# Moving the expert table ahead of the row pick, and a first-freed list of weight buffers, in a transformer block with 32 experts

## The chip, the cores and the metric

The kernel runs on one core of a Trainium2 chip. The metric is the device time of one execution in microseconds. The core's engines are named as in the profile: PE (TensorE, matrix products), DVE (VectorE), ACT (ScalarE), POOL (GpSimd) and SP (SyncE, which here only issues transfers).

## What is computed

Two blocks follow one another on 512 tokens of width 1024, in float32. The first is two layers of windowed attention with a pooling mixer and a gated feed-forward; the second is a recurrent mixer and then a mixture of experts. The change is in the mixture of experts:

```
x = layer_norm(ALPHA * x + mix, ln1_g, ln1_b)
grp = argmax(x @ w_group + b_group)                 # 1 of 4 groups, for each token
top_p, top_i = top_k(softmax(logits of the group's 8 experts), 2)
weights = p_group * top_p / sum(top_p)              # 2 experts for each token
# rows of each expert e, in blocks of up to 128 tokens:
y = (silu(xs @ w1[e]) * (xs @ w3[e])) @ w2[e]       # 1024 -> 512 -> 1024
x = layer_norm(ALPHA * x + sum of weighted y, ln2_g, ln2_b)
```

The three matrices of an expert are 2 MB each, so that the 32 experts hold 201 MB, all of which are read once.

## The kernel before

The first 2000 us compute everything up to the mixer's last product, `mix_out`. It also transposes the result into token rows `XU` (four tiles of 128 tokens), and it issues the loads of the first experts' weights (`prefetch`). `logits` makes the router's scores, `norm1` normalises `XU` on ACT and writes the rows to DRAM (`xs`), `route` chooses the experts.

`route` counts the tokens of each expert, ranks the experts by their count (`perm`, `rr`), and so gets the table `eid`, which says which expert has which rank. Two experts are fixed: ranks 0 and 1 always go to experts 0 and 1 (`NS = 2`), whose weights can therefore be loaded before any token is routed. The other weights are loaded through registers that SP reads from `eid`. Then `table` makes the list of tokens for each expert's 128 places (`tb`), and `weights` the factors of these tokens (`sw`). A large tile R, one-hot over places, is the stationary operand of both.

The experts are worked in 15 units (`UNITS`): ranks 0 to 3 alone, ranks 4 to 19 in pairs of up to 64 tokens, ranks 20 to 31 in fours of up to 32 tokens. Each unit fills the 128 columns of TensorE, so that each takes the same products, while it needs 6, 12 or 24 transfers of 1 MB. `ORDER` is the order of the units. A step of `experts` does, for the next unit n and the present unit u: transposes of n's rows (`xt`), gate product of n (`gu`), `ht` and the down product of u (`yp`), first half of n's up product, `combine` of u into `XU` (`yc`), second half of the up product. Rows of later units come from DRAM by an indirect transfer from POOL (`gather`). The rows of unit 0 are not gathered: `pick`, a 0/1 matrix, is the moving operand of 64 short products (32 in the code, two passes each) with `XU` stationary, which give the rows already transposed; `x_parts` scales them.

Weight tiles (`ew`, 1 MB each) come from pools of several tags. `SLOTS` lists 15 buffers, which are used in turn; the norm's two vectors take one of them until `scale_x` has used them. A phase `rx` holds the tiles of `extra`, a second table for experts with more tokens than their places; after unit 1 that phase is closed, two buffers "n" are opened in its memory, and 17 buffers are used in turn from then on. SP issues the loads in program order, each one as soon as its buffer is free and no more than eight are in flight. The scheduler of the framework orders the other engines' instructions by priority and expected readiness.

After the sixth unit, `overflow` is a loop over the blocks that did not find a place, with a count read at run time. It is empty with these inputs, but all engines go through its entry. Before it, `prefetch` issues transfers for all buffers but one.

Of the kernel before, what the change touches and what calls it, by code (L numbers as in the profile page):

```python
# [20 lines left out]
S = 512  # L21
# [1338 lines left out]
class K3(K2):  # L1360
# [46 lines left out]
    def mix_out(self, H, MH):  # L1407
# [17 lines left out]
        self.tokens(U[7], 7)  # L1425

    def logits(self):
        nc, v = self.nc, self.nc.vector
        T = lambda name, *s: self.ph.tile([128, *s], F32, name=name)
        lt = T("lt", 512)  # L1430
# [29 lines left out]
    def route(self, L):  # L1460
# [39 lines left out]
        self.warm(m, 8)  # L1500
# [8 lines left out]
        xu = self.XU.rearrange("s b (p k) -> s b k p", k=8)  # L1509

        def pick(t, g):
            for b in range(4):
                for i in range(4):
                    nc.tensor.matmul(t[:, i * 128:(i + 1) * 128], lhsT=xu[:, b, 4 * g + i, :], rhs=S[:, b, :],
                                         start=(b == 0 and i == 0), stop=(b == 3 and i == 3))

        X = self.x_parts(pick)

        C = self.keep.tile([128, 5, NE], F32, name="C")
        with self.tc.issue_after(last.ins):  # L1520
# [19 lines left out]
            for n, d in ((SOLO, 64.0), (HALF, 32.0)):  # L1540
# [16 lines left out]
            R, V, V0 = T("R", 8, 128, dt=F32R), T("V", 8, NT, dt=F32R), T("V0", 8, NT)  # L1557
# [3 lines left out]
            v.tensor_tensor(R, iota[:, None, :].to_broadcast([128, 8, 128]), lane[:, :, None].to_broadcast([128, 8, 128]),  # L1561
                            op=OP.is_equal)
# [5 lines left out]
        return X, ga, OH, C  # L1568

    def table(self, R, V, n, nm):  # L1570
# [3 lines left out]
        for i in range(8):  # L1574
            nc.tensor.matmul(p[:, :n], lhsT=R[:, i, :], rhs=V[:, i, :], start=(i == 0), stop=(i == 7))
# [3 lines left out]
        v.tensor_copy(tokf, tok)  # L1579
        return tok, tokf  # L1580

    def slot_weights(self, V0, R, n, nm):

        nc, v = self.nc, self.nc.vector
        w = self.ph.tile([128, 8, n], F32, name="wv" + nm)
        V = self.ph.tile([128, 8, 2, n], F32R, name="wV" + nm)
        h, l = V[:, :, 0, :], V[:, :, 1, :]
# [4 lines left out]
        for i in range(8):  # L1592
            nc.tensor.matmul(p[:, 0:2 * n], lhsT=R[:, i, :], rhs=V[:, i].rearrange("p a b -> p (a b)"), start=(i == 0), stop=(i == 7))
# [5 lines left out]
    def scale_x(self):  # L1599

        gb = [self.part(self.wp["r", "ln1_g_2", "ln1_b_2"], c, D) for c in (0, D)]
        for t in range(4):
            x = self.XU[:, t, :]
            self.nc.vector.scalar_tensor_tensor(x, x, ALPHA, gb[0], op0=OP.mult, op1=OP.mult)
            self.nc.vector.scalar_tensor_tensor(x, gb[1], ALPHA, x, op0=OP.mult, op1=OP.add)

    def weights(self, L, gm, em, V0, R):

        nc, v = self.nc, self.nc.vector
        T = lambda name, *s: self.ph.tile([128, *s], F32, name=name)  # L1610
# [13 lines left out]
        return self.slot_weights(V0, R, NT, "m")  # L1624

    def extra(self, OH, C):

        v = self.nc.vector
        T = lambda name, *s, dt=F32: self.ph.tile([128, *s], dt, name=name)
# [31 lines left out]
        for th in (256.0, 384.0):  # L1661
# [5 lines left out]
        ob1, V, R = T("obx", 8, NX), T("Vx", 8, NX, dt=F32R), T("Rx", 8, 128, dt=F32R)  # L1667
# [4 lines left out]
        v.tensor_tensor(R, iota[:, None, :].to_broadcast([128, 8, 128]), rk[:, :, None].to_broadcast([128, 8, 128]),  # L1672
                        op=OP.is_equal)
        self.xtok, self.xtokf = self.table(R, V, NX, "x")
        self.xws = self.slot_weights(ob1, R, NX, "x")
        yield
        xe, xb, xo = T("xe", NX, NE), T("xb", NX, NE), T("xo", NX)
        io = iota[:, 0:NX, None].to_broadcast([128, NX, NE])
        v.tensor_tensor(xe, io, ovb[:, None, :].to_broadcast([128, NX, NE]), op=OP.is_ge)
        v.tensor_tensor(xb, io, inc[:, None, :].to_broadcast([128, NX, NE]), op=OP.is_lt)  # L1680
        yield
        v.tensor_tensor(xe, xe, xb, op=OP.mult)
        v.tensor_tensor(xe, xe, iota[:, None, 0:NE].to_broadcast([128, NX, NE]), op=OP.mult)
        v.reduce_sum(xo, xe, axis=AX.X)
# [18 lines left out]
    def moe_setup(self):  # L1703
# [15 lines left out]
        self.seq = sum((seq(u, w) for u, w in ((0, 0), (0, 1), (1, 0), (0, 2), (1, 1), (1, 2))), [])  # L1719
        self.seq.append(("r", "ln1_g_2", "ln1_b_2"))  # L1720
# [8 lines left out]
        self.slots = sum(([k] * n for k, n in SLOTS.items()), [])  # L1729
        self.wp, self.nld, self.ev = {}, 0, {}  # L1730

    TAGS = dict(b="rawb", r="raw", w="w", m="m", n="n")
# [28 lines left out]
    def prefetch(self, n=None):  # L1761

        n = self.static if n is None else min(n, len(self.seq))
        while self.nld < n:
            k = self.seq[self.nld]
            r = self.wp[k] = self.slot()
# [6 lines left out]
    def weight(self, u, w):  # L1773

        ks = [(u, w, s, j) for s in range(2) for j in range(UNITS[u][1])]
        self.prefetch(self.seq.index(ks[-1]) + 1)
        return lambda s, j: self.wp[u, w, s, j]
# [37 lines left out]
    def product(self, X, u, m, p=None, ks=range(KB)):  # L1815

        p = p or self.ps("gu")
        w = self.weight(u, m)
# [225 lines left out]
```

## Time and profile before

| | us |
|---|---|
| median of 3 runs | 2572.79 |
| lowest and highest of them | 2572.56, 2578.59 |
| the profiled execution | 2578.66 |
| its span, from the first instruction to the last | 2576.8 |

The span is divided in 40 slices of 64.4 us in the page's slices. Times in the rows are counted from the span's start. The experts begin near 2035 us.

### The profile page before, as it was taken

How to read it: one execution, taken by the hardware profiler on the slowest of the kernel's cores; microseconds unless marked ns; L12 is line 12 of the kernel's file. 1: busy time of each engine (PE TensorE's matmuls, PEld its weight loads, DVE VectorE, ACT ScalarE, POOL GpSimd, SP SyncE). 2: the span in 40 equal slices, each digit the busy share in tenths (PEclk: the TensorE clock that was granted, in tenths of full speed). 3: DMA queues.
4: the chain of work that ended last, by engine and by line, in shares of the span. 5: the costliest groups of instructions: out<-in, count | busy, mean ns of one | idle time of the engine just before them, and what ended most of it. 6: DMA issues, size and time to landing. Idle time of an engine off the chain costs nothing. (4 is left out here: it accounts for less than half of the span.)

```text
span 2576.8 us, 30602 instructions
## 1 busy us (share of the span) xinstructions
PE 2420.7 (94%) x11847; PEld 1774.4 (69%) x11847; DVE 1366.5 (53%) x2190; ACT 906.9 (35%) x1582; POOL 362.7 (14%) x354
## 2 busy tenths in 40 slices
PE   7999999999999999998999999999999888959996
PEld 4678777778788888887878787888887643323332
DVE  4867576437976233346878875455654631122224
ACT  3654232233764222234555554333432211111211
POOL 1334000005342000003423330000000000000000
PEclk9998999999999999999999999999999999979998
DMA  7541675431212332323112222222225469999996
GB/s 254 184 130 57 213 270 196 149 97 51 70 50 74 106 98 83 97 65 99 42 58 74 63 69 93 89 73 89 66 90 208 172 210 420 421 373 420 419 421 253
DMA packets 221295, 416.60 MB, mean 162 GB/s; under 512 B 11619, under 2 KB 185167, under 8 KB 193500
## 3 DMA queue, kind: packets, MB, share of 16 engines
q1 hardware_dynamic: 215472, 408.17, 44.2%
q0 software_dynamic: 2016, 3.73, 0.4%
q10 hardware_dynamic: 3660, 2.72, 0.4%
q8 instruction: 94, 1.54, 0.2%
q14 instruction: 53, 0.43, 0.0%
HBM read 414.01 MB, written 4.19 MB: 162 GB/s over the span
## 5 line engine op out<-in xcount | busy, mean ns | idle before, releaser
L149 DVE TENSOR_TENSOR w<-raw,w 128x1024 fp32r<-128x1024 f32 (+2 forms) x216 | 262.0, 1214 | 231.6 <-ACT w L148 231.6
L148 ACT ACTIVATE w<-raw 128x1024 fp32r<-128x1024 f32 (+2 forms) x228 | 229.0, 1010 | 376.6 <-PE pu L158 148.0
L156 PE MATMUL pj<-Hh,w 128*128 128x512 f32 (+1 forms) x704 | 281.8, 404 | 6.0 <-ACT Hh L392 3.6
L157 PE MATMUL pj<-Hl,w 128*128 128x512 f32 (+1 forms) x704 | 277.7, 396 | 7.4 <-DVE Hl L395 6.8
L158 PE MATMUL pj<-Hh,w 128*128 128x512 f32 (+1 forms) x704 | 274.4, 391 | 0.0
L1812 PE MATMUL gu<-ew,x 128*64 128x512 f32 (+2 forms) x1008 | 238.0, 610 | 7.0 <-DMA ew<-in_w 6.9
L156 PE MATMUL po<-Gh,w 128*128 128x512 f32 (+1 forms) x608 | 212.4, 350 | 0.5 <-ACT Gh L621 0.5
L158 PE MATMUL po<-Gh,w 128*128 128x512 f32 (+1 forms) x608 | 212.1, 349 | 0.0
L157 PE MATMUL po<-Gl,w 128*128 128x512 f32 (+1 forms) x608 | 211.3, 347 | 0.0
L156 PE MATMUL pu<-Hh,w 128*128 128x512 f32 (+1 forms) x448 | 172.1, 384 | 0.2
L158 PE MATMUL pu<-Hh,w 128*128 128x512 f32 (+1 forms) x448 | 170.0, 380 | 0.0
L157 PE MATMUL pu<-Hl,w 128*128 128x512 f32 (+1 forms) x448 | 170.0, 379 | 0.0
L1812 PEld LDWEIGHTS gu<-ew,x 128*64 128x64 f32 (+2 forms) x1008 | 73.1, 136 | 138.7 <-issue 122.9
L157 PEld LDWEIGHTS pj<-Hl,w 128*128 128x128 f32 x704 | 134.9, 192 | 43.4 <-DVE Hl L395 9.7
L158 PEld LDWEIGHTS pj<-Hh,w 128*128 128x128 f32 x704 | 134.3, 191 | 36.6 <-issue 7.7
L156 PEld LDWEIGHTS pj<-Hh,w 128*128 128x128 f32 x704 | 134.5, 193 | 34.7 <-ACT Hh L392 4.7
L1857 DVE SCALAR_TENSOR_TENSOR yl<-yp,wsm,yh 128x512 fp32r<-128x512 f32 x30 | 22.5, 750 | 253.5 <-ACT yh L1856 251.7
L157 PE MATMUL pg<-Hl,w 128*128 128x512 f32 (+1 forms) x384 | 147.2, 384 | 6.7 <-DVE Hl L395 6.6
L156 PE MATMUL pg<-Hh,w 128*128 128x512 f32 (+1 forms) x384 | 147.6, 385 | 0.0
L158 PE MATMUL pg<-Hh,w 128*128 128x512 f32 (+1 forms) x384 | 146.4, 381 | 0.0
L1812 PE MATMUL yp<-ew,hT 128*64 128x512 f32 (+2 forms) x512 | 128.2, 596 | 13.2 <-ACT hT L1838 7.4
L1088 POOL TENSOR_TENSOR QP<-QP,tot 128x512 f32<-128x512 f32 x64 | 102.9, 1611 | 220.9 <-ACT Y L1081 174.5
(508 smaller groups left out, 4763.4 us busy)
## 6 DMA issues: line engine op xcount, KB each, us to landing
ew<-in_w SPq DMA_DIRECT2D x192, 1024.0 KB
raw<-in_w_in SPq DMA_DIRECT2D x34, 1024.0 KB
raw<-in_ada_w SPq DMA_DIRECT2D x24, 1024.0 KB
raw<-in_w_gate SPq DMA_DIRECT2D x22, 1024.0 KB
raw<-in_w_up SPq DMA_DIRECT2D x22, 1024.0 KB
raw<-in_ada_w SPq DMA_DIRECT2D x40, 512.0 KB
raw<-in_w_in SPq DMA_DIRECT2D x40, 512.0 KB
raw<-in_w_down SPq DMA_DIRECT2D x16, 1024.0 KB
```

The lines of the kernel that those rows point to most:

```text
L148: nc.scalar.activation(hv[:, k], rv[:, k], AF.Copy)
L149: (nc.gpsimd if b in self.low else nc.vector).tensor_tensor(lv[:, k], rv[:, k], hv[:, k].bitcast(F32), op=OP.subtract)
L156: nc.tensor.matmul(out, lhsT=wh, rhs=ah, start=first, stop=False)
L157: nc.tensor.matmul(out, lhsT=wh, rhs=al, start=False, stop=False)
L158: return nc.tensor.matmul(out, lhsT=wl, rhs=ah, start=False, stop=last)
L1088: nc.gpsimd.tensor_tensor(w, w, self.other(TOT, h, seg=1), op=OP.mult)
L1812: self.plast = self.nc.tensor.matmul(out[n * j:n * j + n, :], lhsT=X[k // 4][:, k % 4 * 128 + n * j:k % 4 * 128 + n * j + n], rhs=w, start ...
L1857: v.scalar_tensor_tensor(lo, p, ws, hi.bitcast(F32), op0=OP.mult, op1=OP.subtract)
```

## The change

The rows of unit 0 are now picked by 8 products (16 passes) with `pick` stationary and 512 columns of `XU` moving; ACT copies the result to the row buffer `XG[0]`, and the transposes that other units use follow (`x_transpose`). In the program the tables stand ahead of this. The norm's vectors get four tiles of the tag "H" instead of a weight buffer, and so do R (two halves), `lt` and the tiles of `extra`; its phase `rx` is gone. The tag "m" has three buffers, and one "n" is opened when the routing is over. Weight buffers are given out from a list, in the order in which they were freed, and are put on it after each half of a product. The order of the units puts the two fours 12 and 13 behind units 0 and 1. `extra` runs in six steps per unit. Before the loop all 17 buffers are filled.

```diff
-ORDER = (0, 1, 12, 2, 13, 3, 4, 5, 6, 7, 8, 9, 10, 11, 14)
+ORDER = (0, 12, 1, 13, 2, 3, 4, 5, 6, 7, 8, 9, 10, 11, 14)
-SLOTS = dict(b=6, r=3, w=4, m=2)
+FIRST = ["rawb"] * 5 + ["raw"], ["raw"] * 2 + ["w"] * 4
+FREE = ["rawb"] + ["m"] * 3
...
+        self.gb = [self.blk("H", F32, "gb") for _ in range(4)]
+        for i, t in enumerate(self.gb):
+            src = A[("ln1_g_2", "ln1_b_2")[i // 2]]
+            nc.sync.dma_start(t, bass.AP(tensor=src.tensor, offset=src.offset + i % 2 * 512, ap=[[0, 128], [1, 512]]))
...
-        self.warm(m, 8)
+        self.warm(m, 12)
...
-                    nc.tensor.matmul(t[:, i * 128:(i + 1) * 128], lhsT=xu[:, b, 4 * g + i, :], rhs=S[:, b, :],
-                                         start=(b == 0 and i == 0), stop=(b == 3 and i == 3))
-
-        X = self.x_parts(pick)
...
+            R, V, V0 = self.onehot(lane), T("V", 8, NT, dt=F32R), T("V0", 8, NT)
...
-        ga = self.product(X, 0, 0, self.ps("ga", "mod"))
-        with self.tc.issue_after(self.xlast.ins), self.tc.issue_after(self.plast.ins):
             self.tok, self.tokf = self.table(R, V, NT, "m")
             self.ws = self.weights(L, gm, em, V0, R)
+        for i in range(2):
+            p = self.ps("xp")
+            c = slice(i * 512, (i + 1) * 512)
+            for b in range(4):
+                self.plast = nc.tensor.matmul(p, lhsT=S[:, b, :], rhs=self.XU[:, b, c], start=(b == 0), stop=(b == 3))
+            nc.scalar.activation(self.XG[0][:, c], p, AF.Copy)
+        X = self.x_transpose(self.XG[0])
+        with self.tc.issue_after(self.tlast.ins):
             self.scale_x()
...
+    def onehot(self, lane):
+
+        R = []
+        for i in range(2):
+            R.append(self.blk("H", F32R, "R", (128, 4, 128)))
+            self.nc.vector.tensor_tensor(R[i], self.cm[:, None, 0:128].to_broadcast([128, 4, 128]),
+                                         lane[:, 4 * i:4 * i + 4, None].to_broadcast([128, 4, 128]), op=OP.is_equal)
+        return lambda i: R[i // 4][:, i % 4, :]
...
-        self.seq = sum((seq(u, w) for u, w in ((0, 0), (0, 1), (1, 0), (0, 2), (1, 1), (1, 2))), [])
-        self.seq.append(("r", "ln1_g_2", "ln1_b_2"))
+        self.seq = [k for u in range(NS) for w in range(3) for k in seq(u, (0, 1, 2)[w])]
...
-        self.slots = sum(([k] * n for k, n in SLOTS.items()), [])
+        self.free = [s for f in FIRST for s in f] + FREE
...
-    def slot(self):
-
-        self.slots.append(self.slots.pop(0))
-        return self.blk(self.TAGS[self.slots[-1]], F32, "ew", (128, 2048))
+    def slot(self, k=None):
+
+        self.at[k] = self.free.pop(0)
+        return self.blk(self.at[k], F32, "ew", (128, 2048))
+
+    def used(self, u, w, s):
+
+        self.free += [self.at[u, w, s, j] for j in range(UNITS[u][1])]
...
-    def experts(self, X, ga, later, out):
+    def experts(self, X, later, out):
...
-        sub, hT = ExitStack(), None
-        sub.enter_context(self.phase("rx"))
+        hT = None
+        self.free.append("n")
         self.gather(XG[1], col(self.tok, 1))
-        h = self.hidden(ga, self.product(X, 0, 1))
+        h = self.hidden(self.product(X, 0, 0), self.product(X, 0, 1))
...
-            if i < 2:
-                for _ in range(8 if i == 0 else 99):
-                    next(later, None)
-            if i == 1:
-                sub.close()
-                sub.enter_context(self.phase("m2", n=2))
-                self.slots[:0] = ["n", "n"]
+            for _ in range(6):
+                next(later, None)
             if i == QOV:
-                self.prefetch(self.nld + len(self.slots) - 1)
+                self.prefetch(self.nld + len(self.free))
...
-            with self.phase("mo", m=2, HT=1):
+            with self.phase("mo", m=3, HT=1):
...
+                with self.phase("mn", n=1):
+                    self.experts(X, self.extra(*x), out)
```

## Rows read from the trace of the kernel before

**Rows 1.** The page: bytes moved in each slice, and the count of weight transfers.
```profile
GB/s 254 184 130 57 213 270 196 149 97 51 70 50 74 106 98 83 97 65 99 42 58 74 63 69 93 89 73 89 66 90 208 172 210 420 421 373 420 419 421 253
...
ew<-in_w SPq DMA_DIRECT2D x192, 1024.0 KB
```
**Rows 2.** Windows: busy us (instructions) of PE, PEld, DVE, ACT, POOL; clock, DMA share, GB/s.
```profile
2020.00:2030.00 10.00, 10.00 (x43) 10.00 (x44) 0.96 (x4) 1.50 (x4) 0.00 (x0) 1.00 0.00 0
2080.00:2090.00 10.00, 7.68 (x30) 4.63 (x29) 4.33 (x7) 3.38 (x9) 0.99 (x1) 1.00 0.83 302
2100.20:2118.00 17.80, 17.80 (x131) 7.71 (x124) 6.34 (x13) 0.60 (x1) 0.00 (x0) 1.00 0.23 77
2118.00:2294.00 176.00, 136.08 (x532) 52.80 (x530) 31.81 (x52) 21.92 (x49) 2.97 (x3) 0.91 1.00 412
2296.00:2548.20 252.20, 238.17 (x1097) 91.15 (x1095) 63.80 (x103) 42.74 (x96) 6.33 (x7) 0.99 1.00 411
```
**Rows 3.** Timeline of SP: start, duration from first issue to last, count.
```profile
1953.04 47.39 SPq L1759 DMA_DIRECT2D ew<-in_w  x12
2007.70 0.43 SPq L1692 DMA_DIRECT2D ew<-in_ln_b  x1
...
2036.45 64.07 SPq L1759 DMA_DIRECT2D ew<-in_w  x16
...
2117.97 156.65 SPq L1759 DMA_DIRECT2D ew<-in_w  x68
...
2295.90 0.34 SPq L1759 DMA_DIRECT2D ew<-in_w  x1
```
**Rows 4.** SP's waits from 2036 to 2125: us in total, times, longest.
```profile
SPq L1749 <- DVE cap L1539: 18.6, 1, 18.6
SPq L1759 <- PE sw L1593: 16.8, 1, 16.8
```
**Rows 5.** SP's waits from 2255 to 2305, around the loop.
```profile
SPq L1922 <- SPq L1922: 19.2, 5, 9.3
```
**Rows 6.** Timeline of PE at the loop's exit; in brackets its idle time before.
```profile
2294.93 1.97 PE L1803 MATMUL xt<-cst,xg 128*128 128x128 f32 x8 [25.03 <-SPq L1922]
```
**Rows 7.** Timeline of PE and DVE from the pick to unit 1's rows.
```profile
2017.49 1.90 PE L1457 MATMUL warm<-onesb 128*128 128x512 bf16 x8
2019.50 15.48 PE L1514 MATMUL xt<-pick,xu 128*128 128x128 f32 x64
...
2035.05 0.40 PE L1530 MATMUL rr<-cst,rank 32*128 32x32 f32 x2
2035.38 7.13 PE L1812 MATMUL ga<-ew,x 128*128 128x512 f32 x16
...
2047.96 1.36 PE L1575 MATMUL tb<-V,R 128*128 128x16 f32 x8
2049.17 1.04 PE L1593 MATMUL sw<-wVm,R 128*128 128x32 f32 x8
...
2056.79 1.97 PE L1803 MATMUL xt<-cst,xg 128*128 128x128 f32 x8 [5.62 <-DMA xg<-xs,tokm]
...
2020.13 0.23 DVE L1527 TENSOR_SCALAR perm<-cm,rank 32x32 f32<-32x32 f32 x1
...
2035.49 0.18 DVE L1534 CAST eid<-rr 1x32 int32<-1x32 f32 x1 [1.86 <-PE rr L1530]
...
2037.13 1.22 DVE L1604 SCALAR_TENSOR_TENSOR xu<-xu,ew 128x1024 f32<-128x1024 f32 x1
...
2049.77 0.18 DVE L1579 CAST tfm<-tokm 128x16 f32<-128x16 int32 x1
```
**Rows 8.** Chain of waits, one unit of the stretch behind the loop: start, us, what.
```profile
2324.35 1.09 PE xt L1803 x8
...
2333.22 0.60 ACT hT L1838
...
2353.32 1.09 PE xt L1803 x8
```

More of the change, by code (lines that the diff above doesn't have):

```diff
@@ L1592, in slot_weights @@
         for i in range(8):
-            nc.tensor.matmul(p[:, 0:2 * n], lhsT=R[:, i, :], rhs=V[:, i].rearrange("p a b -> p (a b)"), start=(i == 0), stop=(i == 7))
+            nc.tensor.matmul(p[:, 0:2 * n], lhsT=R(i), rhs=V[:, i, :], start=(i == 0), stop=(i == 7))
         ws = self.keep.tile([128, n], F32, name="ws" + nm)
@@ L1599, in scale_x @@
     def scale_x(self):
-        gb = [self.part(self.wp["r", "ln1_g_2", "ln1_b_2"], c, D) for c in (0, D)]
         for t in range(4):
-            x = self.XU[:, t, :]
-            self.nc.vector.scalar_tensor_tensor(x, x, ALPHA, gb[0], op0=OP.mult, op1=OP.mult)
-            self.nc.vector.scalar_tensor_tensor(x, gb[1], ALPHA, x, op0=OP.mult, op1=OP.add)
+            for i in range(2):
+                x = self.XU[:, t, i * 512:(i + 1) * 512]
+                self.nc.vector.scalar_tensor_tensor(x, x, ALPHA, self.gb[i], op0=OP.mult, op1=OP.mult)
+                self.nc.vector.scalar_tensor_tensor(x, self.gb[2 + i], ALPHA, x, op0=OP.mult, op1=OP.add)
     def weights(self, L, gm, em, V0, R):
         nc, v = self.nc, self.nc.vector
-        T = lambda name, *s: self.ph.tile([128, *s], F32, name=name)
+        T = lambda name, *s, dt=F32: self.ph.tile([128, *s], dt, name=name)
         ex, z, d, r = T("ex", 4, 4), T("z", 4), T("dd", 4), T("rr", 4)
@@ L1623, in weights, with T @@
         v.tensor_tensor(W[:, :, 1], W[:, :, 0], d, op=OP.mult)
-        return self.slot_weights(V0, R, NT, "m")
+        return self.slot_weights(V0, R, NT, "m", T)
     def extra(self, OH, C):
         v = self.nc.vector
-        T = lambda name, *s, dt=F32: self.ph.tile([128, *s], dt, name=name)
+        st = {}
+        def T(name, *s, dt=F32):
+            n = math.prod(s)
+            t, o = st.get(dt, (None, 512))
+            if o + n > 512:
+                t, o = self.blk("H", dt, name), 0
+            st[dt] = t, o + n
+            t = t[:, o:o + n]
+            return t.rearrange("p (a b) -> p a b", b=s[-1]) if len(s) == 2 else t
         iota, val, cnt = self.cm[:, 0:128], self.cm[:, 256:264], C[:, 4, :]
@@ L1671, in extra @@
         v.tensor_tensor(V, ob1, val[:, :, None].to_broadcast([128, 8, NX]), op=OP.mult)
-        v.tensor_tensor(R, iota[:, None, :].to_broadcast([128, 8, 128]), rk[:, :, None].to_broadcast([128, 8, 128]),
-                        op=OP.is_equal)
+        R = self.onehot(rk)
         self.xtok, self.xtokf = self.table(R, V, NX, "x")
-        self.xws = self.slot_weights(ob1, R, NX, "x")
+        self.xws = self.slot_weights(ob1, R, NX, "x", T)
         yield
[L1677 to L1684, printed above, removed]
+        xo = T("xo", NX)
+        for h in range(0, NX, 16):
+            xe, xb = T("xe", 16, NE), T("xb", 16, NE)
+            io = iota[:, h:h + 16, None].to_broadcast([128, 16, NE])
+            v.tensor_tensor(xe, io, ovb[:, None, :].to_broadcast([128, 16, NE]), op=OP.is_ge)
+            v.tensor_tensor(xb, io, inc[:, None, :].to_broadcast([128, 16, NE]), op=OP.is_lt)
+            v.tensor_tensor(xe, xe, xb, op=OP.mult)
+            v.tensor_tensor(xe, xe, iota[:, None, 0:NE].to_broadcast([128, 16, NE]), op=OP.mult)
+            v.reduce_sum(xo[:, h:h + 16], xe, axis=AX.X)
+            yield
         self.xtab = self.keep.tile([128, NX + 1], I32, name="xtab")
@@ L1771, in prefetch, with weight @@
             self.nld += 1
-    def weight(self, u, w):
-        ks = [(u, w, s, j) for s in range(2) for j in range(UNITS[u][1])]
+    def weight(self, u, w, s):
+        ks = [(u, w, s, j) for j in range(UNITS[u][1])]
         self.prefetch(self.seq.index(ks[-1]) + 1)
-        return lambda s, j: self.wp[u, w, s, j]
+        return [self.wp[k] for k in ks]
     def gather(self, xg, col):
@@ L1817, in product @@
         p = p or self.ps("gu")
-        w = self.weight(u, m)
         for k in ks:
-            W = [self.part(w(k // 4, j), k % 4 * 512) for j in range(UNITS[u][1])]
+            W = [self.part(r, k % 4 * 512) for r in self.weight(u, m, k // 4)]
             self.rowmm(p, X, k, W, k == 0, k == KB - 1)
+            if k % 4 == 3:
+                self.used(u, m, k // 4)
         return p
@@ L1842, in down @@
         ps = [self.ps("yp"), self.ps("yp")]
-        w = self.weight(u, 2)
         for k in range(4):
             for i in range(2):
-                W = [self.part(w(k // 2, j), k % 2 * D + i * 512) for j in range(UNITS[u][1])]
+                W = [self.part(r, k % 2 * D + i * 512) for r in self.weight(u, 2, k // 2)]
                 self.rowmm(ps[i], h, k, W, k == 0, k == 3)
+            if k % 2:
+                self.used(u, 2, k // 2)
         return ps
@@ L2008, in moe @@
                     self.norm1()
-                    X, ga, *x = self.route(L)
-                self.experts(X, ga, self.extra(*x), out)
+                    X, *x = self.route(L)
+                with self.phase("mn", n=1):
+                    self.experts(X, self.extra(*x), out)
     def run(self, out, ctx):
```

35 lines of the change are left out of this document (11 added, 24 removed).

## The prediction

> **What bounds the kernel now.** I read the page's slices first [rows 1]: the DMA engines are loaded through the last sixth of the span, at some 420 GB/s, while before it they swing between 42 and 270. That last sixth is the 32 experts. The windows by stretch [rows 2] show what to see in it: from 2118 to 2294 and from 2296 to 2548 the engines move 412 and 411 GB/s with a share of 1.00, but from 2020 to 2030 nothing at all, and from 2100 to 2118 only 77 GB/s. So the experts are bound by the transfer of weights wherever it runs, and the question is where it doesn't run. The page counts 192 transfers of 1024 KB, and the SP queue's issues [rows 3] tell when: 12 before the routing, 16 between 2036.45 and 2100.5, 68 from 2117.97 to 2274.6, and 96 after the loop of `overflow`. SP's waits [rows 4] name the two holes: 18.6 us for the table of experts, and 16.8 us for `sw`, the last reader of tiles whose memory the two late "n" buffers take. SP is in order, so everything queued behind that one transfer stood still.
>
> The loop [rows 5, 6] is the gate between the halves. TensorE finishes its work at 2269.9 and idles 25.03 us until SP lets all engines through line 1922, and SP waited there five times, 19.2 us in all: each for one of its transfers in flight to land. So the exit at 2294.93 is the landing of the last transfer issued before the loop, not TensorE's arrival. Bytes check it: 1024 KB are 1.0486 MB; at the 412 GB/s of that stretch (its row gathers included) one takes 2.545 us, 68 take 173.1, and from 2117.97 that leaves 3.9 us for the last landing and the exit. What follows the exit, 2576.8 - 2294.9 = 281.9 us, starts with every buffer full and issues 95 transfers in the same order in both kernels (the 96th of before, at 2295.90, went alone into a buffer that was left empty). I take it as unchanged. The prediction is then the shift of the exit.
>
> **The change part by part.** *The table and the pick.* Now 64 short products build the transposed rows of expert 0 in 15.48 us, and only then the two `rr` products run, though their input `perm` was ready at 2020.36; `eid` follows at 2035.49 [rows 7]. After the change the pick is 8 products of 512 moving columns. The row of `ga` has the same shape and operands, 8 products (16 passes) in 7.13 us. `rr` takes its 0.6 us as soon as `perm` is there, so `eid` comes near 2021.2 and the first dynamic transfer near 2022, 14 us earlier. Then come a copy on ScalarE (0.6 us for the second half, as `hT` in the chain [rows 8]), 8 transposes and 8 scaled copies. Warm-up goes from 8 to 12 products, some 0.24 us each: they end at 2020.3, when nothing but the pick waits, so they cost under 1 us. My sum for expert 0's start: 2020.3 + 0.6 (`rr`) + 7.1 + 0.6 + 1.1 (transposes, as at 2324.35 [rows 8]) + 0.6 until the first scaled columns are there = 2030.3, against 2035.38: 5 us earlier. Bounds: 2029, if half of the transposes' wait is hidden; 2042, if the scheduler puts `tb` and `sw` ahead of the pick and TensorE waits for the lane table. I take the early one, because in before `gu` was placed ahead of `tb`, which stands earlier in the program: the scheduler fills waits.
>
> *Row gathers.* The token table follows `eid` by 14.3 us in before (2035.49 to 2049.77), of which the five 1.22 us operations of `scale_x` between them are moved behind it. So the table is ready near 2031 and the gather for the second expert runs under expert 0's products; the 5.62 us of TensorE's wait for it [rows 7] go. `scale_x` itself becomes 16 halves, and its vectors `gb` come by four transfers of half the size into "H" tiles. They add two issues of 0.4 us on SP at 2007 [rows 3], ahead of the writes of `xs`, which wait for ScalarE's normalised rows anyway. `scale_x` costs nothing as long as it is done before the first `combine`, 30 us later. The one-hot table R, now two halves, has the same columns as now.
>
> *Buffers.* Before: 12 static, one for the norm's rows, two free; two more only after expert 1. After: 12 static, then rawb, m, m, m free, and n as soon as the routing's tiles are dead; freed ones are reused in the order in which they were freed, half by half. So I follow the SP queue. Four transfers go at 2022. n goes when `sw` has been read, near 2035. Expert 0's products run from 2030.3 to 2047.0 (twice 7.13, and 2.4 for `tb` and `sw`) and free four rawb at about 2034, 37, 43 and 47: 21 transfers issued, static ones included. The eight of unit 12's first product have then landed or nearly, it starts at 2049 and frees four buffers at 2052.8. From there more buffers come free than the engines can fill: 4 at 2052.8, 4 at 2056.4, 2 of expert 0's down product by 2065, then 8 from unit 12's second product, 8 from its down product. That is the *order* at work: a unit of four experts hands back 24 buffers in one expert's TensorE time, 29.0 us [rows 8], which is what the engines need 61 us to fill, so the fixed experts on either side of it no longer leave them dry. Full stream from 2052.8.
>
> *The loop.* It waits for 97 transfers instead of 96 (all 17 buffers are filled, not 16): 76 to go. 2052.8 + 76 x 2.545 + 3.9 = 2250.1, against 2294.9: **44.8 us earlier**. TensorE must not be later than that: 2047.0 and six experts at 29.0 us give 2221. The slack of 29 us is what covers all that the change adds elsewhere: the extra table's work in six steps per expert, its tiles in the 16 "H" buffers that experts also use, two halves of `xe`. If that cover were gone, each us more would cost one.
>
> *What is unknown only delays.* If n is free no earlier than `sw` ends now (2050.2), the stream restarts there with 16 issued: 2050.2 + 81 x 2.545 + 3.9 = 2260.2, 10 us less gain. If the third transfer of unit 12's second product gets the rawb of expert 0's down product, free at 2056.4 + 0.6 + 0.6 (`ht` and its copy) + 3.6 = 2061.2, and not the one freed first, the exit is at 2258.5, 8 us less. If the pick comes after the tables, 12 us less. Below, nothing excludes a little more gain: with the stream full from n on (2035, 16 issued) 81 transfers give 2245.0, or 50 us. I take 41, four under the sum, since three of these can only take.
>
> A rate of the Trainium skill speaks against this sum: DMA: Bandwidth & Descriptors, section Where 436 GB/s comes from, has a load from HBM bound at about 358 GB/s for a core. The trace disagrees, with 412 GB/s for 176 us [rows 2]; at 358 the 76 transfers would take 223 us and the gain would be 16.
>
> **The rivals.** *The stream runs slower than I take it.* Between 2080 and 2090 the engines moved 302 GB/s at a share of 0.83 [rows 2], as if full speed were 364: gathers and weights together. If all 76 went so (2.88 us each), the exit is at 2275.6: 19 us gained, 2553 in the median. Against it stand the same gathers inside the 412. Chance 0.06.
>
> *TensorE, not the transfers, reaches the loop last.* The "H" tag has 16 tiles; an expert holds 8 and the next one's rows 2, the extra table some 12 in its time. A wait of the size of the gather's 5.62 us in each of six experts is 34 us, 5 more than the slack. To halve the gain it takes 50 us. Chance 0.14 that something of this kind, or several of the delays above, leaves 8 to 28 us.
>
> *The other side: n is late.* It is now the fifth dynamic transfer, in before the seventeenth, and everything stands behind it on SP. The same kind of wait, for the dead tiles of a phase, took 16.8 us in before. If n came free only where it does in before (2117.8), 81 transfers from there give 2328: 33 us slower, 2606. The sign turns at 2294.9 - 3.9 - 206.1 = 2084.9. For it: the scheduler may put the weights' chain late, as nothing needs `ws` before the first `weighted`. Against it: `sw` follows `tb` by 1.2 us in before. Chance 0.08 for this or another stall that makes it slower.
>
> *No change.* The part behind the loop would have to grow by what is gained before it. It moves 411 GB/s for 252 us, so it is bound by the same 95 transfers, and I see nothing that adds to them. Chance 0.04.
>
> **How the numbers follow.** Measured against the profiled execution (2578.66, of which the span is 2576.8), 41 us less is 2537.7; that execution is 5.9 above the median of the runs (2572.79), with one of three runs as slow. I predict for the median: 2572.8 - 41 = 2532. My case, 28 to 50 us gained, has 0.68 (2523 to 2545); with the smaller gains, 0.20, a range of 2521 to 2556 leaves under 2 in 10 out. By 0.3% (7.7 us), about what these runs can tell from no change: faster 0.88, within 0.04, slower 0.08.
>
> **What would show it.** Right: `rr` before or inside the pick; `eid` near 2021; the pick in about 7 us; first `gu` near 2030; no SP wait over 10 us between 2053 and the loop; DMA share near 1.00 from 2053 on; 97 transfers before the loop and its exit near 2250, with TensorE still waiting some 20 us there; about 282 us after it. Wrong: an SP wait on n or on an "H" reader past 2060; TensorE at the loop last; a stretch behind the loop that is longer.

## The result and the profile after

After the change the median is 2542.44 us (2538.32 to 2547.49, 4 runs), beside it the kernel before ran 2575.69 us: a ratio of 0.9871, 95% interval 0.9846 to 0.9896, so 33 us faster. The forecast was 2532, in a range of 2521 to 2556; it started from the 2572.79 us of three runs of before, which with a fourth became 2575.69. The profiled execution took 2542.54 us with a span of 2540.7, 36.1 less than before's span.

First the windows by stretch of the kernel after; the columns are those of [rows 2].

```profile
2020.00:2030.00 10.00, 10.00 (x54) 4.89 (x53) 6.41 (x41) 2.29 (x5) 0.00 (x0) 1.00 0.15 31
2030.00:2040.00 10.00, 9.05 (x35) 5.53 (x34) 8.68 (x26) 3.60 (x10) 2.42 (x2) 0.83 0.99 417
...
2053.00:2060.00 7.00, 7.00 (x60) 2.37 (x63) 0.10 (x1) 3.28 (x9) 0.99 (x1) 1.00 0.82 259
...
2060.00:2170.00 110.00, 101.20 (x441) 40.11 (x434) 39.78 (x93) 15.47 (x35) 2.97 (x3) 0.97 1.00 413
...
2170.00:2256.00 86.00, 76.85 (x295) 35.58 (x293) 23.50 (x37) 13.77 (x29) 0.99 (x1) 0.97 1.00 411
```

The two holes of before are gone: from 2060 to the loop the DMA engines move 413 and 411 GB/s at a share of 1.00, where before had 0.83 from 2080 to 2090 and 0.23 from 2100 to 2118 [rows 2]. What is left is the dry start (0.15 from 2020 to 2030) and a dent from 2053 to 2060.

The timeline of PE in the kernel after, from the routing to the second expert, and its row at the loop:

```profile
2014.77 0.65 PE L1445 MATMUL lp<-cst,lt 40*128 40x40 f32 x4 [4.93 <-ACT lt L1437]
2015.35 6.74 PE L1463 MATMUL warm<-onesb 128*128 128x512 bf16 x22
2021.92 0.18 PE L1502 MATMUL rk<-Mb,tri 128*128 128x32 bf16 x1
...
2022.54 2.77 PE L1463 MATMUL warm<-onesb 128*128 128x512 bf16 x12
2025.14 1.02 PE L1564 MATMUL xp<-xu,pick 128*128 128x512 f32 x2
2026.09 0.22 PE L1526 MATMUL rr<-perm,cm 32*1 32x32 f32 x2
2026.24 0.40 PE L1527 MATMUL rr<-cst,rank 32*128 32x32 f32 x2
2026.57 6.28 PE L1564 MATMUL xp<-xu,pick 128*128 128x512 f32 x14
2033.24 1.03 PE L1585 MATMUL tb<-V,R 128*128 128x16 f32 x8 [0.40 <-DVE V L1557]
2034.83 1.04 PE L1602 MATMUL sw<-wV,R 128*128 128x32 f32 x8 [0.56 <-DVE tokm L1588]
2035.71 1.73 PE L1824 MATMUL xt<-cst,xg 128*128 128x128 f32 x8
2037.23 15.08 PE L1833 MATMUL gu<-ew,x 128*128 128x512 f32 x32
2052.15 1.05 PE L1824 MATMUL xt<-cst,xg 128*128 128x128 f32 x8
...
2256.82 1.97 PE L1824 MATMUL xt<-cst,xg 128*128 128x128 f32 x8 [6.89 <-SPq L1936]
```

The pick (`xp`) has `rr` inside it, as forecast, and the wait of 5.62 us for the gather is gone: the rows of 2052.15 follow without a pause. But all of it lies later than forecast: the `rk` products start at 2021.92, while before they started at 2016.87, ahead of anything in the change that I had priced. The loop's exit is at 2256.82, against 2294.93 [rows 6]: 38.1 us. SP's waits between 2015 and 2260 in the kernel after:

```profile
SPq L1780 <- PE gu L1833: 105.8, 26, 13.4
SPq L1780 <- PE yp L1833: 33.8, 10, 11.3
...
SPq L1770 <- DVE cap L1536: 9.9, 1, 9.9
SPq L1936 <- SPq L1936: 6.7, 3, 2.8
SPq L1780 <- PE sw L1602: 5.2, 1, 5.2
```

The waits for the table and for `sw` shrank from 18.6 and 16.8 us [rows 4] to 9.9 and 5.2. In their place SP waits for buffers, up to 13.4 us at a time, and these waits cost the stream nothing: the longest lie between 2085 and 2200, where the share is 1.00, since transfers issued earlier are in flight.

The timeline of ACT and DVE in the kernel after shows where the routing is late:

```profile
2011.87 2.37 ACT L1719 ACTIVATE xu<-xu,nmr,lr 128x1024 f32<-128x1024 f32 x2 [0.50 <-DVE nmr L1454]
2014.14 0.57 ACT L1437 ACTIVATE lt<-lg 40x512 f32<-40x512 f32 x1
2014.62 2.36 ACT L1719 ACTIVATE xu<-xu,nmr,lr 128x1024 f32<-128x1024 f32 x2
...
2020.04 0.29 DVE L1495 TENSOR_TENSOR Mb<-OH 128x128 bf16<-128x128 f32 x1
...
2026.68 0.18 DVE L1531 CAST eid<-rr 1x32 int32<-1x32 f32 x1 [1.23 <-PE rr L1527]
```

`lt`, the copy of the router's output, moved by the change into an "H" tile, now stands on ScalarE behind two of the four normalised rows. In before it started at 2010.32, ahead of all four. Everything of the routing waits for it: `lp`, `L`, and at the end `eid`. TensorE ends the router's last product at 2009.83 and ScalarE idles 1.58 us until 2011.07, so it isn't short of time: the copy has a later place in its order. Why the scheduler put it there is not shown.

### The profile page after: what moved, and what is told of

Read it like the earlier page. It is cut to its first block, busy times and chain, and to the rows that moved or that the text cites. A ratio compares the mean times of both kernels' runs of the same rounds, so it can differ in the third digit from the quotient of the medians.

```text
span 2540.7 us, 30559 instructions
## 1 busy us (share of the span) xinstructions
PE 2409.9 (95%) x11811; PEld 1764.5 (69%) x11811; DVE 1369.0 (54%) x2205; ACT 908.0 (36%) x1584; POOL 362.7 (14%) x354
## 5 line engine op out<-in xcount | busy, mean ns | idle before, releaser
L1833 PE MATMUL gu<-ew,x 128*64 128x512 f32 (+2 forms) x1024 | 247.5, 604 | 0.1
L158 PEld LDWEIGHTS po<-Gh,w 128*128 128x128 f32 x608 | 114.5, 188 | 19.1 <-issue 4.2
```

The costliest lines, as they stand in the source:

```text
L158: return nc.tensor.matmul(out, lhsT=wl, rhs=ah, start=False, stop=last)
L1833: self.plast = self.nc.tensor.matmul(out[n * j:n * j + n, :], lhsT=X[k // 4][:, k % 4 * 128 + n * j:k % 4 * 128 + n * j + n], rhs=w, start ...
```

## The experiments

Since the start of the routing itself moves by some 5 us between executions (the router's last product starts between 2005.81 and 2010.87), I read the loop's exit from there as well: it was 285.2 us after that product in before and 247.6 in after. "Exit" below is this distance where it is so marked. One theory stands behind all expectations: the *stream theory*, that the weights' transfers bind the stretch ahead of the loop, so what is late at the first expert, or a hole in the stream, comes out at the exit. Its rivals are named with each.

**Parts undone.** The four kernels ran on one chip, where before took 2579.62 us. The change itself did not run beside them, so their times are compared by the ratio to before, with 0.9871 and the 0.986 of a second measurement below.

The old order of units:

```
-ORDER = (0, 12, 1, 13, 2, 3, 4, 5, 6, 7, 8, 9, 10, 11, 14)
+ORDER = (0, 1, 12, 2, 13, 3, 4, 5, 6, 7, 8, 9, 10, 11, 14)
```

> The changed kernel with only the order of the units put back (0, 1, 12, 2, 13, 3). Stream theory (the loop's exit is set by when the transfer engines become full for good and by how many transfers are left then): the fixed unit 1 follows unit 0, so that TensorE works 28 us on weights that are already there, while only the buffers of unit 0 come free; the engines run dry in that time. I expect the exit some 13 us later than the 2256.8 of the changed kernel and the whole 13 us longer, near 2555, which is still 20 us under the kernel before. Rival (the gain is TensorE's, from the shorter pick and the gather that no longer waits): within 3 us of the changed kernel's 2542.

Measured: 2551.13 us, ratio 0.9892 (0.9875 to 0.9909), exit at 2265.30 and 256.8 after the router. The direction held, the size is below the theory's 13 us: 6 to 9 us of exit, depending on which of two profiles of the change it is set against. Against the 0.9871 the ratio alone would not tell it from the change. The windows of this kernel, and then the one of after, show the place:

```profile
2056.00:2085.00 29.00, 28.09 (x120) 13.48 (x122) 10.76 (x32) 5.37 (x12) 0.99 (x1) 1.00 0.73 238
```

```profile
2056.00:2085.00 29.00, 27.64 (x129) 10.72 (x121) 10.25 (x31) 5.36 (x12) 0.99 (x1) 1.00 0.98 394
```

With the two units of a single expert one behind the other the DMA engines have a share of 0.73 for 29 us, where after has 0.98 and 394 GB/s: 29 x (394 - 238) is 4.5 MB, 11 us of stream at 412, and most of it is missing at the exit.

Fifteen buffers in place of 17:

```
-FREE = ["rawb"] + ["m"] * 3
+FREE = ["rawb"] + ["m"] * 2
-        self.free.append("n")
-            with self.phase("mo", m=3, HT=1):
+            with self.phase("mo", m=2, HT=1):
```

> The changed kernel with two buffers fewer: m has two, and n is not opened, so 15 weight buffers in all. Stream theory: the fifth to eighth dynamic transfers wait for expert 0's buffers instead of going at 2036, the first product of unit 12 stalls some 6 us, and the loop is entered with 95 transfers issued instead of 97. Its exit stays near 2257 (two transfers less make up for the later start), and the two transfers come back behind the loop, 5 us: near 2547. Rival (the two more buffers are the main part of the gain): 15 us or more, above 2557.

Measured: 2550.60 us, 0.9889 (0.9872 to 0.9906), exit at 2259.29, 289.4 us behind it (283.9 in after). From the router the exit is at 250.1, between two profiles of the change (247.6 and, below, 250.9). Held: two buffers are worth little ahead of the loop and some 5 us behind it.

The old pick of 64 short products, everything else as after:

```
-                self.plast = nc.tensor.matmul(p, lhsT=S[:, b, :], rhs=self.XU[:, b, c], start=(b == 0), stop=(b == 3))
-            nc.scalar.activation(self.XG[0][:, c], p, AF.Copy)
-        X = self.x_transpose(self.XG[0])
+                for i in range(4):
+                    nc.tensor.matmul(t[:, i * 128:(i + 1) * 128], lhsT=xu[:, b, 4 * g + i, :], rhs=S[:, b, :],
+                                     start=(b == 0 and i == 0), stop=(b == 3 and i == 3))
+        X = self.x_parts(pick)
```

> The changed kernel with the old pick (64 short products that give the transposed rows), but the tables still ahead of it in the program. The pick takes 15.5 us against 7.3 us and the transposes; the first product of expert 0 starts some 5 us later, near 2042. Stream theory: what is late at the first product is late at the loop, so 5 us more, near 2547. Rival (the pick is hidden behind the transfers of the first dynamic weights, which only come at 2028 to 2050 anyway): within 1 us of 2542. Second rival (the pick is the main part of the gain): 15 us or more.

Measured: 2554.37 us, 0.9902 (0.9884 to 0.9921), exit at 2269.81 and 258.9 after the router. The timeline of PE in this kernel:

```profile
2034.15 1.85 PE L1587 MATMUL tb<-V,R 128*128 128x16 f32 x8 [6.60 <-DVE V L1557]
...
2037.56 15.46 PE L1565 MATMUL xt<-pick,xu 128*128 128x128 f32 x64
2052.85 7.46 PE L1835 MATMUL gu<-ew,x 128*128 128x512 f32 x17
```

The size of the delay missed: the 64 products went behind the tables, and TensorE waited 6.60 us for the lane table first. So the first product came 14.0 us later from the router's last one than in after, and not 5. What was claimed of it held in the main: 8 to 11 us of that, by which of two profiles of the change it is set against, arrive at the exit. This is also the forecast's own bound, "the scheduler puts `tb` and `sw` ahead of the pick and TensorE waits", come true in another kernel.

Fewer transfers ahead of the loop:

```
-                self.prefetch(self.nld + len(self.free))
+                self.prefetch(self.nld + len(self.free) - 6)
```

> The changed kernel with six transfers fewer issued ahead of the loop (11 of the 17 buffers filled). Stream theory: the loop's exit comes near 2251, as soon as TensorE is there, but the engines then stand still from the landing of the 91st transfer, near 2243, until SP goes on at 2252, and the six transfers are moved behind it; from 2252.5 on 101 transfers are left instead of 95 from 2263.7 on, 257 us against 242 at 2.545 us each: 4 us longer in all, near 2546. Rival (TensorE's chain sets the end behind the loop, as the chain of waits says up to 2475): the 6 us of the earlier exit are won, 2536.

Measured: 2546.18 us, 0.9873 (0.9856 to 0.9889). The exit, at 2249.91, came 242.7 us after the router, 4.9 us sooner than in after, and the stretch behind it was 295.4 us instead of 283.9. What is not loaded ahead of the loop is paid behind it, so the wait of 6.89 us at the loop isn't a loss to be won: the rival's 2536 us, a ratio of 0.985, lies outside the interval. The 4 us more that were expected can't be told from none.

**The late copy.** The change once more, and the change with `lt` back in the routing's own memory, on one chip:

```
-        lt = self.blk("H", F32, "lt")
+        lt = T("lt", 512)
```

> The changed kernel unaltered, beside the three that follow. Ratio to the kernel before as measured first, 0.985 to 0.990; the loop's exit 47.6 us after the last router product of the mixer (2009.2 to 2256.8 in its profile).

(The 47.6 us there is a slip for 247.6.) Measured: 2543.60 us, 0.986 (0.9845 to 0.9876), exit 250.9 after the router.

> The changed kernel with the router's scores lt back in the routing's own tiles instead of an H tile. In the changed kernel's trace lt is copied at 2014.14, behind two of the four rows that ScalarE normalises, where it came at 2010.32 before; the count products rk then queue behind the warm-up until 2021.92, 5.0 us later than before. Theory (this is the part of the sum that I missed, and all that follows is late by it): lt within 1 us of the last router product again, rk near 2017, first product of expert 0 near 2032, the loop's exit and the whole 4 to 5 us earlier than the changed kernel. Rival (the transfers are short of buffers in that stretch anyway and set the pace): rk 5 us earlier, but the exit and the whole within 1 us.

Measured: 2536.47 us, 0.9838 (0.9825 to 0.9852), exit 242.0 after the router; repeated below. The timeline of ACT and PE in this kernel:

```profile
2006.44 0.59 ACT L1437 ACTIVATE lt<-lg 40x512 f32<-40x512 f32 x1 [0.38 <-PE lg L1403]
...
2008.55 4.64 ACT L1719 ACTIVATE xu<-xu,nmr,lr 128x1024 f32<-128x1024 f32 x4 [0.62 <-DVE nmr L1454]
...
2007.08 0.44 PE L1445 MATMUL lp<-cst,lt 40*128 40x40 f32 x4 [0.68 <-ACT lt L1437]
2007.45 4.92 PE L1463 MATMUL warm<-onesb 128*128 128x512 bf16 x22
2013.00 0.19 PE L1502 MATMUL rk<-Mb,tri 128*128 128x32 bf16 x1 [0.63 <-DVE Mb L1495]
...
2028.05 14.00 PE L1833 MATMUL gu<-ew,x 128*128 128x512 f32 x32
```

The copy is first on ScalarE again, TensorE waits 0.68 us and not 4.93, and the first product comes 22.2 us after the router's last one instead of 28.0. All five runs of this kernel lie below all four of the change on the same chip, by 7.1 us in the medians, where 4 to 5 were expected. The windows of PE's clock in the two kernels show a second price, after first, then the one with `lt` back:

```profile
2014.70:2022.00 7.30, 7.23 (x29) 3.20 (x30) 4.62 (x34) 3.56 (x4) 0.00 (x0) 0.70 0.69 277
```

```profile
2007.00:2013.00 6.00, 5.29 (x27) 2.40 (x27) 5.65 (x41) 4.78 (x6) 0.00 (x0) 1.00 0.95 376
```

Behind the idle 4.93 us the mean granted clock was 0.70 of 2.4 GHz, part of the stretch at 1.2; the 22 warm-up products took 6.74 us instead of 4.92, outlasted `Mb` (ready at 2020.3) and held `rk` until 2021.92. So 3.8 us of a late copy became 5.0 at `rk`.

**The loop at the end.** Moved from behind the sixth unit to the last but one:

```
-QOV = 5
+QOV = 13
```

> The changed kernel with the loop after the fourteenth unit instead of the sixth, when no transfer of weights is left to issue. Stream theory: the engines no longer stand still around the loop's exit (from 2256 to 2264); full from 2057.1 on, with 172 transfers left (171 weights and the last norm's vectors), the last lands near 2057.1 + 172 x 2.545 + 3.9 = 2499 instead of 2511.5. The loop waits for that landing, and the whole last down product (7.1 us) then stands behind it instead of half of it: 4 to 5 us back. Net 8 us earlier than the changed kernel. Rival (TensorE's chain sets the end): TensorE wins the 6.9 us it waits for the loop, and loses the 4 to 5 again: 2 us.

Measured: 2559.26 us, 0.9923 (0.991 to 0.9937): 15.7 us longer, where 8 less were expected. The theory fails behind the sixth unit. The PE rows that open two successive units there, in the kernel after, then with the loop at the end:

```profile
2315.27 1.16 PE L1824 MATMUL xt<-cst,xg 128*128 128x128 f32 x8
...
2344.36 1.16 PE L1824 MATMUL xt<-cst,xg 128*128 128x128 f32 x8
```

```profile
2343.96 1.16 PE L1824 MATMUL xt<-cst,xg 128*128 128x128 f32 x8
...
2377.82 1.16 PE L1824 MATMUL xt<-cst,xg 128*128 128x128 f32 x8
```

A unit of two experts takes 29.1 us in the one and 33.9 in the other; of the seven steps that follow the loop in after, four take 33.8 to 34.0 us here and two 32.6. By the distance from the router this kernel is 8.6 us ahead where those steps begin, loses 17.3 in them, and 8.3 more behind the last, where it now waits for the loop. The window of this kernel from 2300 to 2500, and PE's waits in it:

```profile
2300.00:2500.00 200.00, 182.44 (x775) 71.43 (x776) 47.98 (x77) 31.32 (x72) 3.96 (x4) 0.97 0.96 380
```

```profile
PE yc L1893 <- DVE sel L1885: 13.5, 6, 2.2
PE ht L1858 <- DVE hs L1850: 5.1, 6, 0.9
```

Neither engine is full: DMA moves 380 GB/s at a share of 0.96, and a unit's twelve transfers at 2.545 us would be 30.5, not 33.9. But TensorE doesn't wait for a transfer in these 200 us: what it lists are 18.6 us of short waits for `sel` and `hs`, against 9.5 and 1.7 us (and 1.5 for `hT`) in the same 200 of after. In the unit from 2343.96 TensorE idles 3.1 us and is busy for 30.8, at a mean granted clock of 0.95; in the one of after from 2315.27 it idles 0.8 and is busy for 28.3, at 1.00. That is the whole difference. The idle time goes with the order of TensorE's instructions, which is fixed before the run (two profiles of one kernel have the same): in the slow unit `combine` follows one pass behind the down product, before its `sel` is ready, in the fast one sixteen. A unit of after with the slow order's two waits and a clock of 1.00, from 2404.03, takes 31.4 us.

So these units are slow by TensorE's order and clock, not by weights that come late. The kernel with six transfers fewer ahead of the loop says the same: from 2336.87 on it has this order too, three units of 33.8 to 33.9 us, and its DMA engines move 418 GB/s meanwhile. What the two kernels share is that TensorE isn't held until all 17 buffers are full, as it is in after. That the scheduler, which orders by expected readiness, chose the order for that reason is a guess; no run shows it.

Both edits together, `lt` back and the loop at the end:

> Both edits together, lt back and the loop after the fourteenth unit. Stream theory: they add up, 12 us under the changed kernel, near 0.983 of the kernel before. Rival: what the one gives the other takes, not more than the better one alone.

Measured: 2551.65 us, 0.9898 (0.9883 to 0.9913). The loop's place costs 15.2 us over `lt` alone moved, as it did without it (15.7): the two edits add, though not to the gain that was expected.

**What is left, on one chip** (before 2580.37 us). The kernel before with nothing but its memory changed: the extra table's tiles in "H" buffers, and the two "n" buffers there from the first expert on. Cut to its core:

```
-        sub.enter_context(self.phase("rx"))
+        sub.enter_context(self.phase("m2", n=2))
+        self.slots[:0] = ["n", "n"]
...
-                sub.close()
-                sub.enter_context(self.phase("m2", n=2))
-                self.slots[:0] = ["n", "n"]
```

> The kernel before, with its order, its pick and its slot rotation, but with the extra table's tiles in the H buffers and the two n buffers there from the first expert on (the phase rx is gone). Theory that the wait of SP for the last reader of the dead tiles (16.8 us before 2117.97) was the largest of the holes in the stream ahead of the loop: that wait goes, the loop's exit comes 12 to 20 us earlier (near 2278), and so does the end: near 0.9935 of the time before. Rival, that order and reuse of buffers make the stream and this wait only stood where another would: exit no more than 5 us earlier, 0.998 to 1.00.

Measured: 2557.78 us, 0.9917 (0.9896 to 0.9938). The exit, at 2273.77 and 267.8 after the router, is 17.5 us earlier than before's by that measure, inside the 12 to 20; the median is 22.6 us lower. SP's waits in this kernel from 2015 to 2300:

```profile
SPq L1779 <- DVE R L1561: 10.6, 1, 10.6
```

So the 16.8 us did go, though "n" now stands first on the queue and holds it for 10.6 us until `R` is done. The first dynamic transfer goes at 2046.64, 10 us later than in before [rows 3] (13.9 by the distance from the router), and the exit is still earlier: the hole at 2100 cost more than this late start.

Only the first of each half product's tiles loaded, and used for all of them (102 of 192 transfers left out; so it computes something else):

```
-                    self.seq += seq(k, w)
+                    self.seq += [x for x in seq(k, w) if x[3] == 0]
...
-        return [self.wp[k] for k in ks]
+        return [self.wp[k]] * UNITS[u][1]
```

> The kernel after, with only the first tile of each half product of a pair or of four experts loaded and used for all of them: 102 of the 192 transfers are left out (what it computes is not the reference's). Theory that the transfers bind the experts and TensorE has about 20 us of slack ahead of the loop: no wait of TensorE for a transfer inside the products, each expert at 27 to 29 us, the loop reached near 2215 to 2230 without a wait over 8 us, 25 us and more before 2256.8, and the end some 40 to 60 us earlier, near 2490. Rival, that TensorE's own work binds: the loop within 10 us of 2256.8 and the end within 20 us of after's.

Measured: 2500.02 us, 0.969 (0.9665 to 0.9715); the loop is left at 2230.75, 26 us before after's, with a wait of 4.07; behind it 266.7 us. The opening rows of PE at the loop and of the next unit:

```profile
2230.75 1.94 PE L1824 MATMUL xt<-cst,xg 128*128 128x128 f32 x8 [4.07 <-SPq L1936]
...
2259.71 1.16 PE L1824 MATMUL xt<-cst,xg 128*128 128x128 f32 x8
```

TensorE reaches the loop at 2226.7, no wait for a transfer is listed on it, and each unit behind takes 29.0 us. The theory's numbers held nearly (43 us of span, 40 to 60 expected). But the run changed two things, for with the transfers TensorE's order changed too. From the first product to the loop TensorE needs 189.1 us here and 212.7 in after, with the same number of products, and after lists no wait for a transfer in them either. Of the 23.6 us, 6.1 are idle time (11.9 against 5.8, for ScalarE and DVE) and 17.5 busy time. The groups of products of four experts in that stretch, in this kernel, then in after:

```profile
L1833 PE MATMUL gu<-ew,x 128*32 128x512 f32 x256 | 31.2, 595 | 0.0
L1833 PE MATMUL yp<-ew,hT 128*32 128x512 f32 x128 | 14.1, 594 | 0.7 <-ACT hT L1860 0.7
```

```profile
L1833 PE MATMUL gu<-ew,x 128*32 128x512 f32 x256 | 40.6, 604 | 0.0
L1833 PE MATMUL yp<-ew,hT 128*32 128x512 f32 x128 | 18.2, 596 | 1.5 <-ACT hT L1860 1.5
```

That is 13.5 of the 17.5 us. Each of these products fills only 32 columns, and four of them run at a time where the four stand side by side in the order. The down product of the first such unit in the timeline of PE, in this kernel, then its second piece in after:

```profile
2091.34 7.07 PE L1833 MATMUL yp<-ew,hT 128*32 128x512 f32 x64 [0.75 <-ACT hT L1860]
```

```profile
2100.45 1.91 PE L1833 MATMUL yp<-ew,hT 128*32 128x512 f32 x4
```

Here 64 take 7.07 us, 0.11 each; in after they come in four pieces between products of the next expert, 11.1 us in all, and in the piece shown four take 1.91, 0.48 each. So the transfers do fill the stretch ahead of the loop in after, with a share of 1.00, but its TensorE has no 20 us to spare, since in its order the same work takes 23.6 us more. How much of the 43 us is the order's and how much the transfers', no run separates.

The slot weights' products behind the first expert's transposes, with `lt` back, and that kernel again beside it:

```
-            self.ws = self.weights(L, gm, em, V0, R)
...
         X = self.x_transpose(self.XG[0])
+        self.ws = self.weights(L, gm, em, V0, R)
```

> The kernel after with lt back in the routing's own memory, and the slot weights' products behind the first expert's transposes instead of ahead of them. Theory that what is late at the first product is late at the exit of the loop: the first product 1.0 to 2.0 us earlier than with lt alone moved (2028.05 there), exit and end as much, 0.983. Rival, that the n buffers, which wait for the slot weights' tiles, then come free later and SP stands there: no gain or up to 3 us longer.

Measured: 2531.95 us (2531.67 to 2537.38), 0.9822 (0.9804 to 0.984), exit 241.3 after the router, the first product 21.2 after it (22.2 with `lt` alone). The rival's condition did not come: the transfer into n goes 20.2 us after the router's last product in both kernels.

> The kernel after with lt back in the routing's own memory, once more beside the two others, since its gain over after (7 us) is near what runs differ by. Both times came from different calls' chips: theory that lt costs 4 to 8 us gives 0.982 to 0.985 of the time before; were the gain chance, 0.987.

Measured: 2539.38 us (2531.59 to 2542.12), 0.9836 (0.9815 to 0.9857), exit 243.1. The gain of `lt` repeats: 0.9838 and 0.9836 against 0.9871 and 0.986 (intervals that overlap at their ends), and the exit is 242.0 and 243.1 against 247.6 and 250.9. Moving the slot weights brings the first product 1.0 us earlier as expected, but its effect on the whole lies inside the intervals. The fastest version of all is the change with both edits, 2531.95 us; that it beats the change is shown for `lt`, not for the second edit.

## Why the prediction came out as it did

The main mechanism was right (the table ahead of the pick, the transfers full from expert 0's end to the loop), and the direction, and the median lies in the range. The sum made the exit 44.8 us earlier and it was 38.1; in the whole, 36.1 us of span came of the 41 that I took, and 33 in the medians. Of the 10.4 us by which 2542.44 lies above 2532, 2.9 are the median of before, which rose with its fourth run. What it had wrong is TensorE's margin at the loop, which cost nothing here. Term by term:

*The first expert's start was the mis-sized term*: 2030.3 forecast, 2037.23 measured. Of the 6.9 us, 5.0 are `rk`, late because of `lt`. The section on the change names the tile and I gave its move no price; I took `rk`'s time over from before. With `lt` back the first product comes 22.2 us after the router's last one, where the forecast makes it 20.6 and after has 28.0. The step from `rk` to `eid` was near (4.3 us forecast, 4.76 measured), the pick too: 7.7 us with `rr` inside, as summed. The other 2 us are the two tables, which the scheduler put ahead of the transposes, with pauses of 0.40 and 0.56 us for DVE. I had argued from before, where `gu` went ahead of `tb`, that they would stand behind; it doesn't carry over. Expert 0's 32 passes took 15.08 us at a clock that dipped, against 14.00 in a profile where it didn't.

*Full stream from 2052.8.* The 22nd issue, which marks it, was at 2057.13: 4.3 us late, and less than the start, since the 2.4 us for `tb` and `sw`, which I had counted behind the first product, stand ahead of it. "n" was free with a wait of 5.2 us on `sw`, near 2035 as forecast. So the rival of a late n did not come; it would have needed 2084.9.

*The rate.* 76 transfers and the last landing took 199.7 us (2057.1 to 2256.8) against 197.3: 2.4 us more. The rate held: 413 and 411 GB/s from 2060 on, gathers included, so the rival of 364 is out. What is missing is that the stream wasn't full at the 22nd issue yet: from 2057.1 to 2060 the engines moved 213 GB/s, which is 1.4 us of the 2.4. The rate of about 358 GB/s that the forecast cited from the Trainium skill (DMA: Bandwidth & Descriptors, Where 436 GB/s comes from) would make an estimated 223 us of it; the trace disagrees here too.

*The loop.* 97 transfers before it, as forecast; TensorE's margin of 20 us isn't there: 6.89. My 2221 is near what TensorE needs in the order that it has with the transfers taken away (2226.7, from a first product as late as after's). But I took 29.0 us per unit from the stretch behind the loop, from units of two experts, and the kernel after has another order ahead of it. TensorE is at the loop at 2249.9, 23 us later, and none of that is listed as a wait for a transfer: the products of four experts alone take 13.5 us longer, where they no longer stand four by four. That each unit takes the same products, as I wrote of the kernel before, holds for their time only while they do. The last two issues, at 2247.5 and 2248.4, wait for buffers that TensorE frees. So transfers and TensorE arrive nearly together, and there was less slack than the prediction counted; that it sufficed is luck in part. The extra table's work is seen in 3.3 us of TensorE's waits (for `ov`, the second `R` and its `wV`).

*Behind the loop* 283.9 us, 2.0 more than before's 281.9. "Unchanged" held within what executions differ by (282.2 to 285.0 in the runs with 17 buffers and the loop in its place).

4.3 + 2.4 + 2.0 = 8.7 us make up the difference between the full sum (span 2532.0) and the 2540.7 measured. The cut of four us for "what is unknown only delays" was the right sign and half of the size. "No SP wait over 10 us" was a wrong test: two kinds reach 13.4 and 11.3 with the engines full.

*Which part gained.* Memory alone gives 17.5 of the 37.7 us by which the exit comes nearer to the router; undoing the pick loses 8 to 11, undoing the order 6 to 9, two buffers next to nothing ahead of the loop, and `lt` takes 5 to 9 us away. These aren't parts of one sum: each is measured with the others in place, the first with the others absent. Two parts that the title names have no run of their own: the table ahead of the pick (the run with the old pick leaves the table where the change put it) and the list of freed buffers in place of the rotation. What each of them gains is not shown.

## What to carry to other kernels

Price every moved tile, also one that only changes its pool: a copy that slips behind two others on its engine delays everything that hangs on it. Where two engines are nearly balanced, look for their floors by taking the work of one away, and compare the order of instructions too: a margin computed for one of them alone, as "TensorE could be there at 2221", holds for the order that it was read from, and here the same products took 183 us of busy time in one order and 201 in another. A stop at which buffers fill needn't be lost time: moving this one to the end cost 15.7 us: the units behind its old place took 17.3 us more, in an order of products with more waits and at a lower clock.

## What I had not expected of the hardware

Ahead of the second expert TensorE's clock fell in two places, and they differ. Behind the idle 4.93 us ahead of `lp` the mean granted clock of the next 7.3 us was 0.65 to 0.73 in each of seven profiles with the late copy, and 1.00 in the three with `lt` back, where that idle time is 0.68. That one goes with the wait in all ten. Around the first expert's first products (0.57 from 2036 to 2040 in after) it doesn't: two profiles of one and the same kernel, the one with `lt` back, had 1.00 there and 0.65, with the same work ahead. It is worth some 1.1 us (15.08 against 14.00 for 32 passes), and what sets it in one execution and not in another stays open. The Trainium skill (TensorE: Matmul & The Clock Gate, Part 1) says that the number of products at the lower clock varies between runs of one kernel; these two profiles agree.

SP can wait 13.4 us for a buffer while the DMA engines stay at a share of 1.00: transfers already issued carry them. The length of a wait on the issuing queue says nothing by itself; the share of the engines beside it decides.
